# The small Pool products of a state-space layer, issued on the vector engine

## The chip, the core and the metric

One core of a Trainium2 chip. The engines that matter here are PE (TensorE, matrix products and transposes), DVE (VectorE), ACT (ScalarE), POOL (GpSimd) and SP, whose queue issues every DMA. Each engine works through its own list of instructions in order and waits on semaphores for the others. The metric is the device time of one execution in microseconds.

## The reference

A trunk of two layers on 1024 tokens of width 1024, in float32. In each layer the normed input is projected once; a slice `u` feeds a state-space (S5) group, the rest a differential attention with four heads. Both are concatenated and projected back, then a convolution-gated feed-forward follows.

```python
h = _rmsnorm(x, norm_mix[i]);  proj = h @ w_in[i]
y_ssm = _s5_group(u, lam_re, lam_im, log_step, b, c, d, w_glu, g_norm)   # 32 groups, 64 states, scan over 1024 tokens
y_att = _diff_attention_group(q, k, v, cos, sin, lam, lam_init, g_subln) # 4 heads, softmax pairs
x = x + jnp.concatenate([y_ssm, y_att], axis=-1) @ w_out[i]
x = x + _conv_gated_ffn(_rmsnorm(x, norm_ffn[i]), w_up[i], w_conv[i], b_conv[i], w_down[i])
```

The scan over tokens is not run step by step. From the poles (`lam_re`, `lam_im`, `log_step`) the kernel works out tables: powers of the pole for steps 0 to 8 times the input and output matrices, and rotations of the pole for 128 blocks of 8 tokens.

## The kernel before

Every float32 product on PE is three reduced-precision products (`mm3`, L399 to L402) on a high and a low part; ACT writes the high part and another engine subtracts it to get the low part. For weights this is `split` (L228 to L233), issued on POOL and giving tiles `op`, from a ring of nine slots (`W`).

At the start of a layer PE runs the projection: products `rw` for attention heads and `u` for the state-space input, in the order of `DENSE`. Beside them a background list (`Tasks`, ticked between groups of products) issues other work:

- `s5_prelude` works out poles and powers (`pt`) and the input matrix `Y` on DVE.
- `s5_rotations` (L634) makes four pairs of tables of 128x1024: products of an index row with the fine (`fl`) and the coarse (`fh`) part of the angle, a reduction to half a turn on DVE, sines on ACT, two stores.
- `s5_tables` (L657) runs 16 batches of two groups. In `first` three operations of 128x288 make `W4` (names `ws<-XC,pt` twice, then `ws<-ws`), six stores follow (`pk`), and three DVE operations of 128x256 make `Gt` (`ws<-Y,pt` twice, then `ws<-ws`). In `second`, one batch later, PE transposes `Gt` (L695, two) and multiplies `Y` by `W4` (L697, two) into a PSUM tile `w`; ACT copies it out, DVE adds `D8`, and `pw` and `kd` are stored.
- After that come the rotary turn of the first head (`ra`, `rb`, `qr`, `kr` on DVE), its transposes (`qt`, `kt`), and attention block by block: scores `sc` on PE, maxima `am` and `anm` on DVE, exponentials `e` on ACT, the weighted difference `e<-e,acf` on DVE, transposes `wt` on PE.

A scheduler under the kernel sets the order on each engine from the program and its own estimates; tiles come from pools of rotating buffers (`s4`: 40 buffers shared by almost all of these names), so that a new tile can wait for readers of an older one. An engine that waits holds up all that stands behind it on that engine.

Of the kernel before, what the change touches and what calls it, by code (L numbers as in the profile page):

```python
# [51 lines left out]
def trunk_kernel(ctx: ExitStack, tc: tile.TileContext, A: dict, out: bass.AP, dbg: dict):  # L52
    nc = tc.nc
    V, G, PE, dma = nc.vector, nc.gpsimd, nc.tensor, nc.sync.dma_start
# [11 lines left out]
    def s4(name):  # L66
        return P4.tile([128, 1024], F32, tag="s4", name=name)
# [10 lines left out]
    def bgt(name):  # L78
        return BG.tile([128, 512], F32, tag="bg", name=name)
# [17 lines left out]
    def act(o, i, f, **kw):  # L97
        return nc.scalar.activation(o, i, f, **kw)  # L98

    def tt(o, a, b, op):  # L100
        V.tensor_tensor(o, a, b, op=op)  # L101

    def ts(o, a, s1, s2, op0, op1):
        V.tensor_scalar(o, a, s1, s2, op0, op1)
# [4 lines left out]
    MUL, ADD, SUB = ALU.mult, ALU.add, ALU.subtract  # L109
# [7 lines left out]
    class Tasks:  # L117
# [3 lines left out]
        def store(self, dst, src):  # L121

            self.late.append((dst, src))
# [384 lines left out]
    def s5_prelude(l, P):  # L508
# [65 lines left out]
        ts(fh, f8, c17, -c17, ADD, ADD)  # L574
        tt(fl, f8, fh, SUB)
        P["rot"] = bg.add(s5_rotations(l, fh, fl, iota))

        Ar, Ai = (pt[:, c:c + 288].rearrange("p (t g) -> p t g", g=32) for c in (0, 288))
# [55 lines left out]
    def s5_rotations(l, fh, fl, iota):  # L634

        for q in range(4):
            p1, p2, p3 = s4("ph1"), s4("ph2"), s4("ph3")
            v1, v2 = (p.rearrange("p (g m) -> p g m", g=8) for p in (p1, p2))
            sh = [128, 8, 128]
            it = iota.unsqueeze(1).to_broadcast(sh)  # L640
            g8 = slice(8 * q, 8 * q + 8)
            G.tensor_tensor(v2, it, fl[:, g8].unsqueeze(2).to_broadcast(sh), op=MUL)
            tt(v1, it, fh[:, g8].unsqueeze(2).to_broadcast(sh), MUL)
            yield
            tt(p3, p1, p2, ADD)
            ts(p3, p3, MAGIC, -MAGIC, ADD, ADD)
            tt(p1, p1, p3, SUB)
            tt(p1, p1, p2, ADD)
            ts(p1, p1, 0.5, -0.5, ALU.min, ALU.max)
            yield  # L650
            act(p2, p1, AF.Abs)
            act(p1, p1, AF.Sin, scale=twopi_s)
            act(p3, p2, AF.Sin, scale=-TWO_PI, bias=halfpi)
            store(rt[l][q][0], p3)
            store(rt[l][q][1], p1)

    def s5_tables(l, P):  # L657
        Ar, Ai, XC, Y, D8 = (P[k] for k in ("Ar", "Ai", "XC", "Y", "D8"))

        def first(b):  # L660
            g2 = slice(2 * b, 2 * b + 2)
            ws = s4("ws")

            We, wt, Gt = ws[:, 0:288], ws[:, 288:576], ws[:, 576:832]
            W4, t4 = (v.rearrange("p (g t c) -> p g t c", g=2, c=16) for v in (We, wt))
            sh = [128, 2, 9, 16]
            ar = Ar[:, :, g2].rearrange("p t g -> p g t").unsqueeze(3).to_broadcast(sh)
            ai = Ai[:, :, g2].rearrange("p t g -> p g t").unsqueeze(3).to_broadcast(sh)
            G.tensor_tensor(W4, XC[:, 0, g2].unsqueeze(2).to_broadcast(sh), ar, op=MUL)
            G.tensor_tensor(t4, XC[:, 1, g2].unsqueeze(2).to_broadcast(sh), ai, op=MUL)  # L670
            G.tensor_tensor(We, We, wt, op=ADD)
            for g in range(2):
                o3 = pk[l][b][:, 128 * g:128 + 128 * g]
                ox = pk[l][b][:, 256 + 128 * g:384 + 128 * g]
                sw = W4[:, g, 1:9, :].rearrange("p t c -> p (t c)")
                store(o3, sw)
                store(ox[0:64], sw[64:128])
                store(ox[64:128], sw[0:64])

            wg = ws[:, 288:544]  # L680
            G4, h4 = (v.rearrange("p (g t c) -> p g t c", g=2, c=16) for v in (Gt, wg))
            sh = [128, 2, 8, 16]
            ar = Ar[:, 7::-1, g2].rearrange("p t g -> p g t").unsqueeze(3).to_broadcast(sh)
            ai = Ai[:, 7::-1, g2].rearrange("p t g -> p g t").unsqueeze(3).to_broadcast(sh)
            tt(G4, Y[:, 0, g2].unsqueeze(2).to_broadcast(sh), ar, MUL)
            tt(h4, Y[:, 1, g2].unsqueeze(2).to_broadcast(sh), ai, MUL)
            tt(Gt, Gt, wg, ADD)
            return b, W4, Gt, wg

        def second(b, W4, Gt, wg):  # L690
            o, q = b // 4, b % 4
            g2 = slice(2 * b, 2 * b + 2)
            ps = bgt("w1")
            for g in range(2):
                PE.transpose(ps[:, 128 * g:128 * g + 128], Gt[:, 128 * g:128 * g + 128], ident)  # L695
            for g in range(2):
                PE.matmul(ps[0:16, 256 + 128 * g:384 + 128 * g], Y[:, 0, 2 * b + g, :],  # L697
                          W4[:, g, 0:8, :].rearrange("p t c -> p (t c)"), start=True, stop=True)
            W1 = PW.tile([128, 2, 192], F32, tag="W1", bufs=3, name="W1")
            act(W1[:, :, 0:128], ps[:, 0:256].rearrange("p (g n) -> p g n", g=2), AF.Copy)  # L700
            act(W1[:, :, 128:192], ps[:, 0:256].rearrange("p (g n) -> p g n", g=2)[:, :, 0:64], AF.Copy)
            store(pw1[l][b], W1.rearrange("p g n -> p (g n)"))
            kp = wg[0:16].rearrange("p (g n) -> p g n", g=2)
            act(kp, ps[0:16, 256:512].rearrange("p (g n) -> p g n", g=2), AF.Copy)
            tt(kp[:, :, 0:16], kp[:, :, 0:16], D8.rearrange("p (g c) -> p g c", c=16)[:, g2, :], ADD)
            store(kd[l][o][:, 2 * q:2 * q + 2, 128:256], kp)

        held = []
        for b in range(16):
            held.append(first(b))  # L710
            yield
            if len(held) > 1:
                second(*held.pop(0))
        while held:
            yield 1
            second(*held.pop(0))
# [780 lines left out]
```

## Time and profile before

| | us |
|---|---|
| median of 3 runs | 2598.11 (2595.41 to 2607.71) |
| profiled execution | 2603.88 |
| its span, first to last instruction | 2602.1 |

| engine | busy, us | share of the span |
|---|---|---|
| PE | 2357.7 | 91% |
| DVE | 1747.9 | 67% |
| POOL | 1245.9 | 48% |
| ACT | 1131.7 | 43% |

The profile page gives busy time over the whole run; the stages differ. The two layers repeat each other: what stands at 62 to 220 us in the first layer stands at 1346 to 1490 us in the second. Times in the rows are microseconds from the start of the span. In a row of the chronological view the columns are start, length, engine, line, operation, output<-inputs, count, and in brackets how long the engine sat idle before it and who released it. An instruction's length there includes time in which it had started and could not proceed.

### The profile page before, as it was taken

The numbers are of one execution on the slowest core, as the hardware profiler recorded it, in microseconds if no ns is written. First come the engines' busy times: TensorE is split into PE (matmuls) and PEld (weight loads), VectorE is DVE, ScalarE is ACT, GpSimd is POOL, SyncE is SP. The second block draws the span as 40 slices with busy tenths as digits, with TensorE's granted clock in tenths as the row PEclk, the third lists the DMA queues.
The fourth block names the chain that finished last, engine by engine and source line by source line (L and its number), as shares of the span: only waits on it lengthen the run. The fifth ranks groups of instructions, "written<-read, shape, count | busy, mean of one in ns | idle before, by whom it ended". The sixth has DMA issues, their size and how long they took to land. (4 is left out here: it accounts for less than half of the span.)

```text
span 2602.1 us, 34422 instructions
## 1 busy us (share of the span) xinstructions
PE 2357.7 (91%) x12180; PEld 1948.0 (75%) x12180; DVE 1747.9 (67%) x3145; ACT 1131.7 (43%) x2164; POOL 1245.9 (48%) x957
## 2 busy tenths in 40 slices
PE   6689999997999999787996898999989999979888
PEld 5667987776888887566786688877768888866666
DVE  7977657758444444899588875676674444469985
ACT  4355346434544444333334542653344444433331
POOL 2741001026777776766237310011467777765761
PEclk8889999998999999899998999999999999999999
DMA  5334641321323223431234357214122322252311
GB/s 164 107 108 123 183 128 45 134 88 57 90 73 97 73 84 112 153 130 65 74 98 138 98 139 207 82 49 150 65 73 73 97 74 81 90 200 92 105 42 65
DMA packets 269828, 266.99 MB, mean 103 GB/s; under 512 B 40280, under 2 KB 227256, under 8 KB 269656
## 3 DMA queue, kind: packets, MB, share of 16 engines
q1 hardware_dynamic: 269656, 264.79, 32.8%
q8 instruction: 96, 1.57, 0.2%
q14 instruction: 76, 0.62, 0.1%
HBM read 188.17 MB, written 76.55 MB: 102 GB/s over the span
## 5 line engine op out<-in xcount | busy, mean ns | idle before, releaser
L232 POOL TENSOR_TENSOR op<-st,op 128x512 fp32r<-128x512 f32 x112 | 163.8, 1480 | 703.5 <-ACT op L98 661.3
L232 POOL TENSOR_TENSOR op<-wu,op 128x512 fp32r<-128x512 f32 x220 | 286.9, 1314 | 266.5 <-ACT op L98 266.2
L107 DVE SCALAR_TENSOR_TENSOR c<-u,cv,c 128x1023 f32<-128x1023 f32 (+1 forms) x176 | 227.2, 1291 | 61.9 <-ACT c L98 57.0
L400 PE MATMUL rw<-op,hTh 128*128 128x256 f32 x768 | 231.4, 301 | 5.4 <-ACT hTh L98 3.5
L232 POOL TENSOR_TENSOR op<-wd,op 128x512 fp32r<-128x512 f32 x106 | 156.1, 1489 | 161.7 <-ACT op L98 151.9
L401 PE MATMUL rw<-op,hTh 128*128 128x256 f32 x768 | 227.7, 296 | 1.2 <-POOL op L232 1.2
L402 PE MATMUL rw<-op,hTl 128*128 128x256 f32 x768 | 226.1, 295 | 0.0
L400 PE MATMUL dnc<-op,aop 128*128 128x512 f32 x360 | 155.7, 434 | 77.2 <-DVE xf L101 74.8
L101 DVE TENSOR_TENSOR u<-u,upc 128x512 f32<-128x512 f32 x88 | 60.1, 683 | 234.6 <-ACT u L98 234.5
L232 POOL TENSOR_TENSOR op<-w,op 128x512 fp32r<-128x512 f32 x124 | 170.0, 1390 | 41.1 <-ACT op L98 36.2
L98 ACT ACTIVATE op<-wu 128x512 fp32r<-128x512 f32 x220 | 138.0, 629 | 97.2 <-PE upd L402 57.6
L400 PEld LDWEIGHTS rw<-op,hTh 128*128 128x128 f32 x768 | 154.4, 201 | 9.3 <-ACT hTh L98 3.9
L400 PEld LDWEIGHTS dnc<-op,aop 128*128 128x128 f32 x360 | 71.9, 200 | 117.5 <-DVE xf L101 95.3
L401 PEld LDWEIGHTS rw<-op,hTh 128*128 128x128 f32 x768 | 154.5, 201 | 2.9 <-POOL op L232 2.0
L402 PEld LDWEIGHTS rw<-op,hTl 128*128 128x128 f32 x768 | 154.4, 201 | 1.1 <-issue 1.0
L98 ACT ACTIVATE op<-wd 128x512 fp32r<-128x512 f32 x106 | 66.5, 631 | 198.6 <-PE dnc L402 140.1
L101 DVE TENSOR_TENSOR xf<-xf,dnc 128x512 f32<-128x512 f32 (+1 forms) x160 | 123.8, 788 | 43.1 <-PE dnc L402 42.0
L98 ACT ACTIVATE u<-upa 128x512 f32<-128x512 f32 x132 | 78.6, 596 | 168.0 <-PE upa L402 168.0
L401 PE MATMUL dnc<-op,aop 128*128 128x512 f32 x360 | 148.4, 412 | 0.0
L402 PE MATMUL dnc<-op,aop 128*128 128x512 f32 x360 | 145.7, 413 | 1.1 <-DVE aop L232 1.0
L98 ACT ACTIVATE c<-u,cv 128x1024 f32<-128x1024 f32 x88 | 106.4, 1211 | 32.5 <-DVE u L101 29.7
L915 DVE TENSOR_REDUCE am<-sc 128x1 f32<-128x256 f32 (+7 forms) x128 | 94.3, 751 | 32.8 <-PE sc L913 32.5
(342 smaller groups left out, 7276.7 us busy)
## 6 DMA issues: line engine op xcount, KB each, us to landing
wu<-in_w_up_dram SPq DMA_DIRECT2D x88, 512.0 KB, 4.8
gd<-g SPq DMA_DIRECT2D x44, 512.0 KB, 3.1
wd<-in_w_down_dram SPq DMA_DIRECT2D x44, 512.0 KB, 4.2
g<-gd SPq DMA_DIRECT2D x44, 512.0 KB, 5.6
st<-in_w_in_dram SPq DMA_DIRECT2D x32, 256.0 KB, 4.4
st<-in_w_in_dram SPq DMA_DIRECT2D x16, 512.0 KB, 4.7
rt<-ph SPq DMA_DIRECT2D x16, 512.0 KB, 3.6
C<-rt SPq DMA_DIRECT2D x64, 128.0 KB, 2.8
```

The lines of the kernel that those rows point to most:

```text
L98: return nc.scalar.activation(o, i, f, **kw)
L101: V.tensor_tensor(o, a, b, op=op)
L107: return V.scalar_tensor_tensor(o, a, s, b, op0, op1)
L232: eng.tensor_tensor(lo.bitcast(F32R), src, hi, op=SUB)
L400: PE.matmul(o, l[0], r[0], start=first, stop=False, skip_group_check=go_on)
L401: PE.matmul(o, l[0], r[1], start=False, stop=False, skip_group_check=go_on)
L402: PE.matmul(o, l[1], r[0], start=False, stop=last, skip_group_check=go_on)
L915: V.tensor_reduce(out=m[:, c:c + 1], in_=sv, axis=AX.XY, op=ALU.max)
```

## The change

Four lines issue their operation on DVE instead of POOL: the product with the fine angle part in `s5_rotations` (four a layer, 128x1024) and the three operations that make `W4` in `s5_tables` (48 a layer, 128x288). In all 104 instructions change engine; what is computed is the same.

```diff
@@ s5_rotations
-            G.tensor_tensor(v2, it, fl[:, g8].unsqueeze(2).to_broadcast(sh), op=MUL)
+            tt(v2, it, fl[:, g8].unsqueeze(2).to_broadcast(sh), MUL)
             tt(v1, it, fh[:, g8].unsqueeze(2).to_broadcast(sh), MUL)
@@ s5_tables, first
-            G.tensor_tensor(W4, XC[:, 0, g2].unsqueeze(2).to_broadcast(sh), ar, op=MUL)
-            G.tensor_tensor(t4, XC[:, 1, g2].unsqueeze(2).to_broadcast(sh), ai, op=MUL)
-            G.tensor_tensor(We, We, wt, op=ADD)
+            tt(W4, XC[:, 0, g2].unsqueeze(2).to_broadcast(sh), ar, MUL)
+            tt(t4, XC[:, 1, g2].unsqueeze(2).to_broadcast(sh), ai, MUL)
+            tt(We, We, wt, ADD)
```

Since the scheduler places instructions anew, the order on the engines shifts with it. On DVE, in the first layer, around the first batch (`ws_1166`; `ph1_1134`, `ph2_1135`, `ph3_1136` belong to the second rotation table):

```order
-L101 TENSOR_TENSOR ws_1166<-Y_1021,pt_621 128x256 x2
+L101 TENSOR_TENSOR ws_1166<-XC_820,pt_621 128x288 x2
+L101 TENSOR_TENSOR ws_1166<-Y_1021,pt_621 128x256
+L101 TENSOR_TENSOR ws_1166<-ws_1166 128x288
 L101 TENSOR_TENSOR ph3_1136<-ph1_1134,ph2_1135 128x1024
+L101 TENSOR_TENSOR ws_1166<-Y_1021,pt_621 128x256
+L104 TENSOR_SCALAR ph3_1136<-ph3_1136 128x1024
 L101 TENSOR_TENSOR ws_1166<-ws_1166 128x256
```

The three new operations stand between and ahead of those that make `Gt`, for which PE's transposes wait. On PE the transposes of a batch move behind more products of the projection (`w1_1258` is the PSUM tile of the first batch, `rw_1225` a projection tile):

```order
-L695 MATMUL w1_1258<-ident_78,ws_1166 128x128 x2
-L697 MATMUL w1_1258<-ws_1166,Y_1021 16x128 x2
 L400 MATMUL rw_1225<-op0_314,hTh_511 128x256
...
 L400 MATMUL rw_1225<-op2_320,hTh_529 128x256
+L695 MATMUL w1_1258<-ident_78,ws_1166 128x128 x2
+L697 MATMUL w1_1258<-ws_1166,Y_1021 16x128 x2
 L401 MATMUL rw_1225<-op2_320,hTh_529 128x256
```

They stand 13 products later than before, those of the second and third batch 39 and 58 products later; when the first `qt` comes, PE has passed six batches in both orders. In the second layer 49 products more stand ahead of the first `qt` than before. A third place is DVE's list after the change at the first attention block (`am_1840`, `anm_1841`), where the thirteenth batch (`ws_1901`) stands:

```order
L915 TENSOR_REDUCE am_1840<-sc_1851 128x1
L101 TENSOR_TENSOR ws_1901<-XC_820,pt_621 128x288 [waits Pool_49]
L104 TENSOR_SCALAR anm_1841<-am_1840 128x1 [waits DVE_49]
L101 TENSOR_TENSOR ws_1901<-XC_820,pt_621 128x288
L101 TENSOR_TENSOR ws_1901<-Y_1021,pt_621 128x256
L101 TENSOR_TENSOR ws_1901<-ws_1901 128x288 [waits DVE_49]
```

Here the buffer that `ws_1901` gets was last read by a split on POOL, so DVE waits for POOL with the block's `anm` behind it; before, the waits for buffers of `ws` stood on POOL.

## Rows read from the trace of the kernel before

**Rows 1.** Windows: PE, PEld, DVE, ACT, POOL busy (instructions), clock, DMA share, GB/s

```profile
62.00:140.00 78.00, 53.20 (x367) 48.07 (x367) 72.65 (x139) 26.65 (x58) 57.72 (x48) 0.85 0.33 99
140.00:171.30 31.30, 24.21 (x166) 20.05 (x166) 25.50 (x54) 15.54 (x38) 15.41 (x17) 0.92 0.36 110
171.30:220.00 48.70, 47.77 (x265) 36.58 (x266) 38.02 (x105) 30.46 (x84) 11.53 (x12) 0.94 0.36 100
1346.50:1415.00 68.50, 48.21 (x330) 43.52 (x328) 64.33 (x112) 24.06 (x49) 52.27 (x35) 0.86 0.29 97
1415.00:1450.00 35.00, 29.87 (x218) 25.80 (x217) 29.53 (x55) 18.23 (x45) 20.29 (x21) 0.99 0.34 109
```

**Rows 2.** Waits of PE (60:300, 1360:1600: total, times, longest); two chronological PE rows

```profile
PE w L695 <- DVE ws L101: 22.0, 5, 8.1
...
PE w L695 <- DVE ws L101: 20.3, 5, 7.5
...
89.52 0.69 PE L695 MATMUL w<-ident,ws 128*128 128x128 f32 x2 [8.11 <-DVE ws L101]
...
171.34 0.48 PE L943 MATMUL wt<-ident,e 128*128 128x128 f32 x1 [3.81 <-DVE anm L104]
```

**Rows 3.** Chronological rows of POOL, then of DVE, 62 to 67 us

```profile
61.96 1.94 POOL L642 TENSOR_TENSOR ph<-D,pt 128x1024 f32<-128x1024 f32 x1 [23.67 <-DVE am L104]
64.75 1.89 POOL L642 TENSOR_TENSOR ph<-D,pt 128x1024 f32<-128x1024 f32 x1
...
62.03 1.91 DVE L101 TENSOR_TENSOR t<-am,lrt 128x32 f32<-128x32 f32 x1
63.97 2.72 DVE L101 TENSOR_TENSOR pt<-pt 128x32 f32<-128x32 f32 x1
```

**Rows 4.** Chronological rows of DVE beside an idle POOL

```profile
89.99 0.41 DVE L101 TENSOR_TENSOR ws<-Y,pt 128x256 f32<-128x256 f32 x1
90.33 1.21 DVE L101 TENSOR_TENSOR ph<-ph,ph 128x1024 f32<-128x1024 f32 x1
```

**Rows 5.** DVE groups: 62:171 (three), 28:62 (one), 1346.5:1450 (two); whole run (min/median/max)

```profile
L101 DVE TENSOR_TENSOR ws<-Y,pt 128x256 f32<-128x256 f32 x26 | 14.2, 563 | 1.8 <-POOL ws L671 1.5 <-PE qt L858 0.2
L107 DVE SCALAR_TENSOR_TENSOR r<-rd_k,r 128x32 f32<-128x32 f32 x18 | 11.0, 610 | 0.2
...
L104 DVE TENSOR_SCALAR nl<-nl 128x1 f32<-128x1 f32 x1 | 0.1, 141 | 0.0
...
L107 DVE SCALAR_TENSOR_TENSOR r<-rd_k,r 128x32 f32<-128x32 f32 x4 | 0.8, 192 | 0.1
...
L101 DVE TENSOR_TENSOR ws<-Y,pt 128x256 f32<-128x256 f32 x26 | 18.7, 737 | 6.3 <-POOL ws L671 4.6 <-PE qt L858 1.2 <-issue 0.3
L101 DVE TENSOR_TENSOR ph<-ph,ph 128x1024 f32<-128x1024 f32 x12 | 18.3, 1522 | 0.0
...
L101 DVE TENSOR_TENSOR ws<-Y,pt x64: 405/414/1514, 86.2 to 1469.7; 128x256 f32<-128x256 f32 x64
```

**Rows 6.** POOL groups of 62:171 and 1346.5:1450: the splits; one split beside little else

```profile
L232 POOL TENSOR_TENSOR op<-st,op 128x512 fp32r<-128x512 f32 x11 | 22.5, 2060 | 7.8 <-ACT op L98 7.7
...
L232 POOL TENSOR_TENSOR op<-st,op 128x512 fp32r<-128x512 f32 x12 | 21.3, 1788 | 8.3 <-ACT op L98 8.3
...
1498.87 1.27 POOL L232 TENSOR_TENSOR op<-st,op 128x512 fp32r<-128x512 f32 x1 [2.60 <-ACT op L98]
```

**Rows 7.** Chronological rows of POOL: its longest waits ahead of a batch's first product

```profile
143.07 0.70 POOL L669 TENSOR_TENSOR ws<-XC,pt 128x288 f32<-128x288 f32 x1 [7.65 <-DMA kd<-ws]
156.06 0.94 POOL L669 TENSOR_TENSOR ws<-XC,pt 128x288 f32<-128x288 f32 x1 [10.52 <-PE qt L858]
183.69 0.70 POOL L669 TENSOR_TENSOR ws<-XC,pt 128x288 f32<-128x288 f32 x1 [8.30 <-PE wt L943]
...
1433.23 0.94 POOL L669 TENSOR_TENSOR ws<-XC,pt 128x288 f32<-128x288 f32 x1 [8.76 <-PE qt L858]
1461.14 0.70 POOL L669 TENSOR_TENSOR ws<-XC,pt 128x288 f32<-128x288 f32 x1 [8.13 <-DMA st<-in_w_in_dram]
```

## Prediction before the run

> **What bounds the kernel now.** I read the busy times first, then the windows of the stage that holds the changed lines, then PE's waits, then DVE and POOL side by side. Over the run PE is busy 91%, so a gain must come from time in which PE stands still. In the stretch where the tables are made PE is busy only 53.2 of 78.0 us, and in the second layer 48.2 of 68.5, while DVE is busy 72.7 and 64.3 [rows 1]. Right behind, from 171 to 220 us, PE is busy 47.8 of 48.7 [rows 1]: there PE is the bound. PE's waits name the reason: transposes L695 for a batch's `Gt` wait for DVE, 22.0 us in the first layer and 20.3 in the second, five waits each; the first is 8.1 us, and the last wait of this stage that DVE causes is for the weighted difference at 171.3 us [rows 2]. So **DVE's list, from 62 to 171 us and from 1346 to 1450 us, sets the pace**, and the sum has to be made on DVE.
>
> Much of DVE's busy time there is no work. At 62.03 us a product of 32 columns lasts 1.91 us and ends at 63.94; POOL's product L642 beside it runs from 61.96 to 63.90. The next one to show it, at 63.97, lasts 2.72 us and ends at 66.69, with POOL's second L642 ending at 66.64 [rows 3]. Such a small product takes about 0.19 us where POOL is idle. DVE is held while POOL has an operation in flight.
>
> **The change part by part.**
>
> *What DVE gets.* Lengths overlap by 0.07 us: the 256-column product at 89.99 lasts 0.41 and the next starts 0.34 later [rows 4]. No row shows 288 columns on DVE. From 0.34 a step for 256 columns and 1.21 - 0.07 = 1.14 for 1024 [rows 4] a column costs (1.14 - 0.34)/768 = 1.04 ns, and 288 columns 0.37 us. By the first weighted difference DVE's new list has passed 13 of the 16 batches and all four angle products: 39 x 0.37 = 14.4 and 4 x 1.14 = 4.6, **19.0 us a layer**. The bounds are close: 0.34 and 0.44 a step (the latter if nothing overlaps) give 17.8 and 21.7.
>
> *What DVE loses.* I compare each group of DVE instructions in the window 62 to 171 with its length where POOL is idle. The 18 steps `r` of the angle reduction average 610 ns against 192: 7.5 us. The 26 products `ws<-Y,pt` average 563 against a median of 414: 3.9 us. Done for all 55 groups of this window, from the largest down to the single `nl` step of 141 ns, the excess is **34.4 us**. In the second layer the same comparison gives 34.1, with 26 x (737 - 414) = 8.4 from `ws<-Y,pt` and 12 x (1522 - 1210) = 3.7 from `ph<-ph,ph` as its first terms (1210 being the 128x1024 step of rows 4) [rows 4, 5]. POOL is busy 57.7 + 15.4 = 73.1 us in these stretches of the first layer, 22.5 of them with splits that stay; in the second 72.6 and 21.3 [rows 1, 6]. If the holding goes by POOL's busy time, 69% and 71% of it leave with the moved operations: **23.8 and 24.2 us**. DVE's own waits for `ws` from POOL, 1.5 and 4.6 us [rows 5], go too, because producer and consumer then share a list.
>
> *The sum on DVE.* First layer 19.0 - 23.8 - 1.5 = -6.3; second 19.0 - 24.2 - 4.6 = -9.8; together **-16.1 us**. PE follows it one to one as long as it waits for DVE in these stretches, which is where it loses time now; its new order lets it do 13 to 58 products before a transpose that waited, so that nothing on PE itself stands against it. Its clock is at 0.85 of full there, between the two levels 1.2 and 2.4 GHz; I give that no term, since a PE that waits for DVE gains nothing by running faster between waits.
>
> *Behind that point.* Three batches a layer are left, 9 x 0.37 = 3.3 us on DVE, where DVE is busy 38.0 of 48.7 us and PE nearly always [rows 1]: between 0 and 3.3 a layer, I take 1, so +2 in all.
>
> *POOL's waits that come along.* A batch's first product waits until its buffer is free. On POOL that cost nothing: 7.65, 10.52 and 8.30 us in the first layer, 8.76 and 8.13 in the second, 43.4 together [rows 7]. On DVE such a wait holds the rotary turn, the maxima and the differences queued behind. It costs between 0 and 43.4. I take 0: POOL ran ahead of DVE, while DVE reaches these batches later by itself, and in the new order the tenth batch's wait for `qt` stands behind DVE work that needs the same `qt`.
>
> *POOL's gain* is worth nothing by itself: the splits for weights run up to nine slots ahead of PE, and the waits of PE in rows 2 are not for them.
>
> Sum: -16.1 + 2 = **-14 us**. The profiled execution took 2603.88 us (span 2602.1 and 1.8 around it), 5.8 above the median of 2598.11; it becomes about 2590, and the median 2584.
>
> One rule is weighed here. The split of the holding above rests on busy time; the two rows at 62 us show a DVE product held to the end of POOL's operation. The Trainium skill, "SBUF — State Buffer", section "Who interferes with whom", says that a DVE instruction with two SBUF inputs and a POOL instruction that reads SBUF exclude each other, and that the second to issue blocks fully until the first ends. The rows at 62 us agree [rows 3]. By that rule taken in full each remaining split could hold DVE for its whole length when alone, 1.27 us: 11 and 12 splits give 14.0 and 15.2 us in place of the 10.6 and 9.9 that I leave standing, and the sum would be -14 + 8.7 = -5 us, 2593.
>
> **The rivals.**
>
> *A. Little is left of it* (2593; -2 to -10 us). The splits stay and find a DVE with more two-input products to collide with; if each holds DVE for its full 1.27 us, 8.7 us of the gain are lost, as worked out from rows 6. For it: POOL's splits already last 2060 and 1788 ns on average against 1.27 alone, so they meet DVE often. Against it: of the 73.1 us POOL is busy, DVE's excess is only 34.4, so a POOL operation costs DVE less than its length.
>
> *B. Slower: the buffer waits move onto DVE* (2608). The place is the first attention blocks: the thirteenth batch waits for a split on POOL, that one for ACT and for PE to be done with a ring slot, and `anm` stands behind it; the ninth to fourteenth batches wait for stores of earlier ones, which share SP's queue. If DVE meets a bit more than half of the 43.4 us [rows 7], some 24 us, the total is -14 + 24 = +10. From 14 us of such waits on the change loses. Against it: all of these waits end by things that themselves run behind DVE.
>
> *C. More: PE's waits go almost entirely* (2560). The new order puts 58 products ahead of the third batch's transposes and 49 more ahead of the second layer's first `qt`. If the waits at L695, 42.3 us [rows 2], nearly all go, the total is -38. Against it: DVE's list, at 19.0 us more work, still has to pass before the rotary turn.
>
> *D. It does not do what it says* (2635). If DVE's excess is not POOL's doing, 19.0 us are added twice and little is taken away: 38 + 2, less 0 to 6.1 of DVE's waits for `ws`, is +34 to +40. The rows at 62 us speak against it [rows 3].
>
> **How the numbers follow.** Forecast, -10 to -25 us: 0.45, at 2584. A: 0.26. B: 0.15. C: 0.11. D: 0.03. A measurement of this kernel tells a difference of about 0.5%, 13 us, from none. The forecast lies mostly beyond that (seven parts in ten, 0.32), and with C, 0.11, makes 0.43 for faster. Slower by over 13 us are D and half of B, 0.03 + 0.08 = 0.11. The rest, 0.46, is within the bound: A, the other half of B and the smaller values of the forecast. The likeliest single value stays 2584, just beyond the bound. The range, 2566 to 2606, takes in the forecast, A, the lower part of B and the nearer part of C; left out are some 0.07 of C, 0.09 of B and D's 0.03. The bounds of the unknown costs fit: the price of 288 columns moves the sum by -2 to +6, the last three batches by -2 to +5.
>
> **What would show it.** Right, if in the changed profile the 18 steps `r` average under 400 ns, the new `ws<-XC,pt` products take about 0.44 us, PE's waits at L695 fall below 15 us a layer, and the first one below 4; POOL's busy time falls by about 117 us while DVE's changes by less than 15. A is it if the steps `r` stay near 500 ns beside splits. B is it if DVE shows idle times before `ws<-XC,pt` released by POOL, PE or a DMA. C is it if PE is busy over 65 of the 78 us. The prediction is wrong at its root if DVE's excess stays with POOL nearly empty, or if PE stands idle elsewhere by as much as it gains here.

## The result

The changed kernel took 2573.05 us (median of 4 runs, 2572.01 to 2576.36); the kernel before, beside it on the same chip, took 2601.59 us (4 runs, 2595.41 to 2607.71). The ratio is 0.9886, with a 95% interval from 0.9869 to 0.9904: 28.5 us less, clear of the 0.5% that a measurement of this kernel can tell from no change. The profiled execution's span fell from 2602.1 to 2571.4 us. The sign and the range held; the size, -14 us, was half of what came, which lies beyond the forecast's -10 to -25 us and short of rival C's -38.

### The profile after

The windows of the changed kernel, cut at the same events as in [rows 1] (the first rotary transposes, the first `wt`), columns as there; the last two rows are the second layer's:

```profile
62.00:128.60 66.60, 51.18 (x376) 46.41 (x375) 63.89 (x176) 28.70 (x61) 35.05 (x16) 0.87 0.32 102
128.60:156.10 27.50, 26.44 (x175) 21.86 (x174) 26.41 (x68) 16.29 (x40) 6.19 (x4) 0.95 0.42 132
156.10:205.00 48.90, 45.43 (x262) 35.78 (x263) 39.77 (x118) 31.10 (x83) 5.11 (x4) 0.97 0.39 106
1331.00:1396.20 65.20, 50.71 (x380) 47.31 (x379) 56.56 (x146) 26.95 (x56) 34.06 (x8) 0.88 0.31 102
1396.20:1423.00 26.80, 25.72 (x175) 21.73 (x173) 25.68 (x65) 16.61 (x40) 6.23 (x4) 0.97 0.41 129
```

The stage of the first layer, 109.3 us long before, now takes 94.1. DVE, with 39 more products of 288 columns and 4 of 1024 in it, is busy for 90.3 us where it was busy for 98.2: it does more work in less busy time. The groups of the first layer's stage (62 to 156 us), columns as in [rows 5]:

```profile
L101 DVE TENSOR_TENSOR ws<-XC,pt 128x288 f32<-128x288 f32 x26 | 11.9, 474 | 0.0
L101 DVE TENSOR_TENSOR ws<-Y,pt 128x256 f32<-128x256 f32 x26 | 10.4, 409 | 0.1
L101 DVE TENSOR_TENSOR ph<-D,pt 128x1024 f32<-128x1024 f32 x8 | 9.6, 1207 | 0.0
L107 DVE SCALAR_TENSOR_TENSOR r<-rd_k,r 128x32 f32<-128x32 f32 x18 | 4.3, 236 | 0.0
```

The steps `r` average 236 ns against 610 before, `ws<-Y,pt` 409 against 563, and no idle time stands ahead of the new `ws<-XC,pt`. PE's waits in the two stages (60 to 300 us, then 1330 to 1600; total, times, longest):

```profile
PE w L695 <- DVE ws L101: 15.4, 5, 4.8
...
PE rw L401 <- POOL op L232: 10.0, 1, 10.0
...
PE w L695 <- ACT ph L98: 1.9, 1, 1.9
```

In the first layer the waits for `ws` fell from 22.0 to 15.4 us. In the second they are nearly gone (20.3 before), but a wait stands there that the trace of before does not have: 10.0 us for a split on POOL (before, no wait of PE for a split of the projection was over 0.7 us). The reason is in the group of POOL's splits, first layer and second:

```profile
L232 POOL TENSOR_TENSOR op<-st,op 128x512 fp32r<-128x512 f32 x12 | 41.0, 3442 | 63.7 <-ACT op L98 63.7
...
L232 POOL TENSOR_TENSOR op<-st,op 128x512 fp32r<-128x512 f32 x12 | 40.3, 3391 | 60.1 <-ACT op L98 60.1
```

With almost nothing else on POOL a split lasts 3.4 us, longer than the 2060 and 1788 ns of [rows 6], and 1.27 alone. The chronological rows of the second layer show one of them (POOL, then DVE beside it, then PE):

```profile
1352.65 9.34 POOL L232 TENSOR_TENSOR op<-st,op 128x512 fp32r<-128x512 f32 x1 [34.19 <-ACT op L98]
1361.95 12.41 POOL L232 TENSOR_TENSOR op<-st,op 128x512 fp32r<-128x512 f32 x1
...
1352.57 0.67 DVE L104 TENSOR_SCALAR ph<-ph 128x1024 f32<-128x1024 f32 x1
1353.17 0.41 DVE L101 TENSOR_TENSOR ws<-ws 128x256 f32<-128x256 f32 x1
...
1359.63 1.20 DVE L101 TENSOR_TENSOR ph<-D,pt 128x1024 f32<-128x1024 f32 x1
1360.76 1.27 DVE L101 TENSOR_TENSOR ws<-ws,D 16x32 f32<-16x32 f32 x1
...
1366.95 0.17 DVE L101 TENSOR_TENSOR ws<-ws,D 16x32 f32<-16x32 f32 x1
...
1372.03 1.21 DVE L101 TENSOR_TENSOR ph<-D,pt 128x1024 f32<-128x1024 f32 x1
...
1374.42 0.58 PE L401 MATMUL rw<-op,hTh 128*128 128x256 f32 x1 [10.04 <-POOL op L232]
```

From 1352.57 to 1360.76 DVE runs 13 instructions back to back at their undisturbed lengths, and the split that started at 1352.65 ends only at 1361.99. In its last 1.2 us it is DVE that is held: an add of 32 columns, 0.17 us at 1366.95, lasts 1.27. So POOL got its turn only at this add, after 8 us. The next split waited the same way: the add at 1366.95 did not let it in, DVE ran out of work at 1373.24, the split ended at 1374.36, and PE stood behind it. The holding works both ways: before, a busy POOL held DVE; now an unbroken DVE holds POOL.

To count it, each instruction of the stage (62 us to the first `wt`; the second layer's likewise) is compared with the length that 15% of its group (same operation and shape, in the two traces together) stay under. What it lasts longer is DVE's excess; beside it stands DVE's idle time (gaps of over 0.15 us), in us:

| kernel | excess, layer 1 | excess, layer 2 | idle, layer 1 | idle, layer 2 |
|---|---|---|---|---|
| before | 34.8 | 34.0 | 10.3 | 9.1 |
| changed | 7.8 | 3.8 | 3.2 | 9.1 |

### The profile page after: what moved, and what is told of

Same layout as the page of the kernel before. It is cut to its first block, busy times and chain, and to the rows that moved or that the text cites. A ratio compares the mean times of both kernels' runs of the same rounds, so it can differ in the third digit from the quotient of the medians.

```text
span 2571.4 us, 34399 instructions
## 1 busy us (share of the span) xinstructions
PE 2348.4 (91%) x12180; PEld 1945.3 (76%) x12180; DVE 1725.8 (67%) x3249; ACT 1134.1 (44%) x2164; POOL 1168.7 (45%) x853
## 5 line engine op out<-in xcount | busy, mean ns | idle before, releaser
L232 POOL TENSOR_TENSOR op<-st,op 128x512 fp32r<-128x512 f32 x112 | 199.8, 1806 | 850.1 <-ACT op L98 782.1
L401 PE MATMUL rw<-op,hTh 128*128 128x256 f32 x768 | 226.0, 294 | 10.5 <-POOL op L232 10.5
L400 PE MATMUL rw<-op,hTh 128*128 128x256 f32 x768 | 227.9, 297 | 6.9 <-ACT hTh L98 3.5
L401 PEld LDWEIGHTS rw<-op,hTh 128*128 128x128 f32 x768 | 151.9, 198 | 13.0 <-POOL op L232 11.3
L98 ACT ACTIVATE e<-sc,anm 128x256 f32<-128x256 f32 (+7 forms) x128 | 93.8, 736 | 49.4 <-DVE anm L104 36.3
```

Of the source, the lines that this page charges most:

```text
L232: eng.tensor_tensor(lo.bitcast(F32R), src, hi, op=SUB)
L400: PE.matmul(o, l[0], r[0], start=first, stop=False, skip_group_check=go_on)
L401: PE.matmul(o, l[0], r[1], start=False, stop=False, skip_group_check=go_on)
```

## The experiments

The theory: a POOL operation in flight holds DVE, so what the change gains is the holding that leaves, less the work that DVE gets. The rivals: the gain comes from the new order (the three products and their readers on one list, the transposes later on PE), or the splits that stay set the rest.

### One part alone

`e1_angle` issues only L642 on DVE:

```diff
-            G.tensor_tensor(v2, it, fl[:, g8]..., op=MUL)
+            tt(v2, it, fl[:, g8]..., MUL)
```

> Only the angle product L642 goes to DVE (8 instructions in all); the three W4 products stay on POOL. Theory of holding (a POOL product in flight holds DVE): 18.0 of the 116.7 us of moved POOL time leave, 15 percent of the 57 us of excess that the whole change removed, 9 us; DVE gets 8 x 1.14 = 9 us of work: no difference, 2595 to 2607. Theory of order (the gain comes from W4 and its reader standing on one list): no difference either. A gain of 10 us or more would say that a few long POOL operations hold DVE for more than their share.

Measured: 2597.82 us, ratio 0.9976 (0.9963 to 0.9988), beside 2604.09 of before: -6 us, within the expected 2595 to 2607.

`e2_w4` issues only L669 to L671 on DVE.

> Only the three W4 products go to DVE (96 instructions); L642 stays on POOL. Theory of holding: 85 percent of the 57 us of excess leave, 48 us, the work added is 78 x 0.37 = 29 us, DVE's waits for ws go (6 us): -25 us, about 2577. If L642 is what holds DVE most, at the stage's start: -15 us or less, 2587 or more.

Measured: 2578.91 us, ratio 0.9900 (0.9880 to 0.9919): -25 us. That is what the theory of holding expected. Together the parts give -31 us, about the whole; the angle product gives a fifth of it, with 15% of the moved POOL time. The steps `r` in the stage, for the first and the second kernel:

```profile
L107 DVE SCALAR_TENSOR_TENSOR r<-rd_k,r 128x32 f32<-128x32 f32 x18 | 8.3, 461 | 0.1
...
L107 DVE SCALAR_TENSOR_TENSOR r<-rd_k,r 128x32 f32<-128x32 f32 x18 | 5.4, 302 | 0.0
```

610, 461, 302, 236 ns: the less POOL does, the shorter DVE's small steps. The order theory has no reason for that, but it is not excluded by these two.

### The four products left out

`e4_left_out` is the kernel before without them: W4's stores and products read a piece of `Y`, and the rotations add the index row.

```diff
-            G.tensor_tensor(v2, it, fl[:, g8]..., op=MUL)
...
-            tt(p3, p1, p2, ADD)
+            tt(p3.rearrange("p (g m) -> p g m", g=8), v1, it, ADD)
...
-            G.tensor_tensor(W4, XC[:, 0, g2]..., ar, op=MUL)
-            G.tensor_tensor(t4, XC[:, 1, g2]..., ai, op=MUL)
-            G.tensor_tensor(We, We, wt, op=ADD)
```

> The kernel before with the four POOL products left out: W4's stores and products read a piece of Y, the rotations add the index row instead of the fine part. Theory of holding: DVE is free of the moved operations and has no work for them; the steps r average under 250 ns; of the 38 us that these products cost DVE in the changed kernel it gains what PE's remaining waits in the two stages allow, 15.4 + 15 = 30 us: 2540 to 2550. Theory of order, with no holding: DVE's work is that of before, only its waits for ws (6 us) go: 2592 to 2602.

Measured: 2552.71 us, ratio 0.9804 (0.9788 to 0.9820). That is 51 us less than before, 3 us short of the 2540 to 2550 that the theory of holding expected; the order theory's 2592 to 2602 is far off. Against the changed kernel's ratio of 0.9886 the difference is 0.8%, some 21 us: what the 38 us of products cost when DVE does them. So the operations on POOL cost 51 us, on DVE 21, each with what hangs on them (the stores of `pk` no longer wait for them). The steps `r` missed the expected 250 ns, at 366, and the excess was 10.5 and 8.0 us, more than in the changed kernel. The splits last 2327 ns there in the first layer, where they last 3442 in the changed kernel: beside fewer products on DVE they get in sooner. Why they do was not isolated.

### One-input copies in place of the products

`e5_pool_copy` keeps four POOL operations of the same size, but as copies (the second factor and the sum are left out):

```diff
-            G.tensor_tensor(v2, it, fl[:, g8]..., op=MUL)
+            G.tensor_copy(v2, fl[:, g8]...)
...
-            G.tensor_tensor(We, We, wt, op=ADD)
+            G.tensor_copy(We, wt)
```

> The kernel before with the four POOL products replaced by POOL copies of the same size with one input (the second factor and the sum are left out). If any POOL operation in flight holds DVE, by its busy time: the steps r stay at 500 to 600 ns and the time follows the copies' busy time, 2585 to 2605 if they are about as long as the products. If only operations with two inputs on both engines exclude each other: r falls to 200 to 260 ns, and the time is near that of the kernel without the products, 2540 to 2560.

Measured: 2574.36 us, ratio 0.9884 (0.9868 to 0.9899), `r` at 338 ns, between the two expectations. The chronological rows tell why (POOL, then DVE):

```profile
62.79 1.09 POOL L642 COPY ph<-pt 128x1024 f32<-128x1024 f32 x1 [24.52 <-DVE am L104]
63.82 0.94 POOL L502 MEMSET zero<- 16x1024 f32 x1
64.72 1.03 POOL L642 COPY ph<-pt 128x1024 f32<-128x1024 f32 x1
...
62.87 1.05 DVE L101 TENSOR_TENSOR t<-am,lrt 128x32 f32<-128x32 f32 x1
63.84 0.17 DVE L101 TENSOR_TENSOR t<-am,lit 128x32 f32<-128x32 f32 x1
63.95 1.84 DVE L101 TENSOR_TENSOR pt<-pt 128x32 f32<-128x32 f32 x1
```

A copy with one input holds DVE just as long as it lasts; it is only shorter, 1.03 us for 1024 columns where the product of [rows 3] took 1.89 to 1.94. So it is not a matter of two inputs on POOL. The product at 63.95 is held through the MEMSET, which reads nothing, and the copy behind it; the one at 63.97 in [rows 3] began beside the same MEMSET and was held through the product behind it. A MEMSET with nothing behind it is found in the changed kernel (POOL, then DVE); the last two rows are the same DVE instructions in `e4_left_out`, with POOL idle:

```profile
46.86 0.94 POOL L502 MEMSET zero<- 16x1024 f32 x1 [9.06 <-DVE hn L107]
...
47.26 0.28 DVE L101 TENSOR_TENSOR lamv<-lamv 128x128 f32<-128x128 f32 x1
47.45 0.43 DVE L104 TENSOR_SCALAR gs<-gs 128x128 f32<-128x128 f32 x1
...
47.47 0.28 DVE L101 TENSOR_TENSOR lamv<-lamv 128x128 f32<-128x128 f32 x1
47.67 0.22 DVE L104 TENSOR_SCALAR gs<-gs 128x128 f32<-128x128 f32 x1
```

The product with two inputs takes 0.28 us beside the MEMSET as without it; the TENSOR_SCALAR is held until the MEMSET ends. The Trainium skill, "SBUF — State Buffer", section "Who interferes with whom", says that a DVE instruction with two SBUF inputs doesn't contend with a GpSimd instruction that only writes. The row at 47.26 agrees, and the product at 63.84 above passed beside the MEMSET too. The rows at 63.95 and 63.97 don't settle it, since in both a POOL operation with inputs follows the MEMSET at once; what held these two products from their start stays open.

### POOL made busy again

Is it POOL's activity by itself? `e6_extra_pool` adds to the changed kernel four POOL products a batch that nobody reads, in spare columns of `ws`:

```diff
+            for _ in range(4):
+                G.tensor_tensor(ws[:, 832:1024], xf[:, 0:192], xf[:, 192:384], op=MUL)
             tt(G4, Y[:, 0, g2]..., ar, MUL)
```

> The changed kernel with four POOL products of 128x192 a batch added whose results nobody reads: same work and same order of dependences on DVE, only POOL is busy again (64 a layer, some 30 us). Theory of holding, POOL over DVE: DVE's steps r are back at 400 us or more in ns, the excess rises by the added POOL time of the stage, some 20 us a layer, and the time to 2600 to 2615. Theory that DVE's unbroken stream keeps POOL out: the added products stretch instead, DVE's lengths stay, and the time is 2573 to 2585, with longer waits of PE for splits queued behind them. Theory of order: no difference, 2573.

Measured: 2614.76 us, ratio 1.0041 (1.0026 to 1.0056). The time went where the theory of holding had it, but not by its way alone: `r` stood at 256 ns. The groups of the first layer's stage, DVE and POOL, then chronological rows of POOL and one of DVE:

```profile
L101 DVE TENSOR_TENSOR ws<-XC,pt 128x288 f32<-128x288 f32 x26 | 13.1, 520 | 9.8 <-POOL op L232 9.8
L107 DVE SCALAR_TENSOR_TENSOR r<-rd_k,r 128x32 f32<-128x32 f32 x18 | 4.6, 256 | 0.0
...
L687 POOL TENSOR_TENSOR ws<-XC 128x192 f32<-128x192 f32 x55 | 57.5, 1053 | 17.9 <-ACT XC L98 14.8
...
110.53 16.91 POOL L687 TENSOR_TENSOR ws<-XC 128x192 f32<-128x192 f32 x1
...
135.35 28.65 POOL L687 TENSOR_TENSOR ws<-XC 128x192 f32<-128x192 f32 x34
163.96 5.37 POOL L232 TENSOR_TENSOR op<-st,op 128x512 fp32r<-128x512 f32 x4
...
165.26 1.50 DVE L101 TENSOR_TENSOR ws<-XC,pt 128x288 f32<-128x288 f32 x1 [9.78 <-POOL op L232]
```

DVE's excess rose to 17.2 and 22.2 us, but beside it stand waits for POOL ahead of `ws<-XC,pt`, 9.8 and 8.3 us: in the first layer the split that DVE waits for stands on POOL behind 34 of the added products. It is the prediction's rival B, made by hand. The run doesn't tell the two apart, so a second one adds POOL work without that tie: in `e7_extra_own` two products a batch write spare columns of `D8`'s tile (`pad`), and nothing on DVE needs them.

```diff
+            for _ in range(2):
+                G.tensor_tensor(P["pad"], xf[:, 0:192], xf[:, 192:384], op=MUL)
             tt(G4, Y[:, 0, g2]..., ar, MUL)
```

> The changed kernel with two POOL products of 128x192 a batch added (32 a layer, 0.6 us each, 19 us) whose result goes to spare columns that nobody reads, so that no work on DVE waits for them; they run in one row from the moment XC is there (62 us). Theory of holding, POOL over DVE: in the first 25 us DVE's lengths grow by most of the 19 us, the first transposes of the stage come 10 to 19 us later than in the changed kernel (84.5 us), and the time is 2595 to 2611. Theory that DVE's stream keeps POOL out: the added products stretch to over 1 us on average, DVE's excess grows by under 6 us a layer, and the time rises only by what splits queued behind cost: 2575 to 2590.

Measured: 2598.85 us, ratio 0.9983 (0.9974 to 0.9993). PE's waits in the first layer (L698 is the changed kernel's L695), POOL's row, and DVE's small steps beside it:

```profile
PE w L698 <- DVE ws L101: 26.7, 5, 15.7
...
62.44 29.42 POOL L687 TENSOR_TENSOR D<-XC 128x192 f32<-128x192 f32 x29 [23.91 <-ACT XC L98]
...
63.18 0.59 DVE L101 TENSOR_TENSOR t<-pt,lrt 128x32 f32<-128x32 f32 x1
64.37 0.17 DVE L104 TENSOR_SCALAR pt<-t 128x32 f32<-128x32 f32 x1
65.24 0.58 DVE L104 TENSOR_SCALAR pt<-t 128x32 f32<-128x32 f32 x1
```

DVE's work and its order are the changed kernel's, instruction by instruction; only POOL is busy with some 19 us a layer that nobody needs (32 products of 0.59 us at the shortest). The first transposes of the stage come at 99.04 us in place of 84.46, DVE's excess is 23.1 and 22.9 us in place of 7.8 and 3.8, and almost the whole gain of the change is gone: 25 us. That is the holding measured by itself. With the new order but a busy POOL only 3 us of gain are left, so the order alone is not the reason. It may still have a part: DVE's idle time is 2.3 and 1.2 us here, where before had 10.3 and 9.1. With the holding that left (34.8 - 23.1 and 34.0 - 22.9) this about pays for the 19.0 us of work that DVE gets in each layer. Whether the order or DVE's longer list took these waits away was not separated.

### The splits that stay

`e3_split_dve` issues the twelve splits of the stage on DVE too (`plain` gets an engine: the second head's and both state-space parts):

```diff
-                plain([(wcols(w, 0, 8, 256 * i, 256), 0)])
+                plain([(wcols(w, 0, 8, 256 * i, 256), 0)], V)
...
+                      V if i == 1 else G)
```

> The changed kernel with the weights' splits of three projection parts (the second head and both state-space parts, 12 a layer, those that POOL runs in the table stage) issued on DVE as well. In the changed kernel they last 3.4 us on average on POOL, DVE's stream keeps them out, and PE waits 10.0 us for one in the second layer. Theory that the holding is mutual and that a held split is what is left: PE's 10.0 us go, DVE's rest of excess (7.8 and 3.8 us) goes, and DVE gets 12 x 0.62 = 7.4 us a layer: 2560 to 2568. Theory that POOL's splits are hidden and PE would have waited for DVE anyway: the added 7 us a layer come out in full, 2580 to 2588.

`e3b_split_h1` does so for the second head's four alone, among them the one for which PE waited.

> The changed kernel with only the second head's four splits a layer on DVE, among them the one for which PE waited 10.0 us. Mutual holding: PE's wait goes, DVE gets 4 x 0.62 = 2.5 us a layer: 2562 to 2569, as good as moving all twelve or better. If PE's wait only moves to the transposes behind it: 2573 to 2578.

`after_again` is the changed kernel beside them.

> The changed kernel once more, on the same chip as the others of this set, as their measure: 2570 to 2577.

Measured: 2561.61 us for all twelve (ratio to before 0.9841, 0.9824 to 0.9857; the theory that a held split is what is left had 2560 to 2568), 2576.63 for the four (0.9893, 0.9877 to 0.9910), 2573.36 for the changed kernel (0.9881, 0.9866 to 0.9895). All twelve on DVE bring 12 us more and make the fastest kernel that computes the reference here: DVE's excess falls to 1.6 and 1.4 us, its idle time to 1.3 and 0.9. A split takes there (group of the first layer's stage) 0.68 us, about half of its 1.27 on an undisturbed POOL:

```profile
L232 DVE TENSOR_TENSOR op<-st,op 128x512 fp32r<-128x512 f32 x10 | 6.5, 675 | 0.2 <-ACT op L98 0.2
L107 DVE SCALAR_TENSOR_TENSOR r<-rd_k,r 128x32 f32<-128x32 f32 x18 | 3.1, 175 | 0.0
```

The four alone brought nothing, against the theory's 2562 to 2569: the wait moved, as the other expectation had it, and the way is worth following. Second layer, POOL's splits; the wait of SP's queue; ACT; PE:

```profile
1362.63 30.73 POOL L232 TENSOR_TENSOR op<-st,op 128x512 fp32r<-128x512 f32 x3 [1.52 <-ACT op L98]
...
SPq L331 <- POOL op L232: 10.6, 1, 10.6
...
1398.34 0.55 ACT L98 ACTIVATE W<-w 128x256 f32<-128x256 f32 x2 [7.98 <-DMA pw<-W]
...
1399.19 1.11 PE L868 MATMUL kt<-ident,kr 128*128 128x128 f32 x4 [7.92 <-ACT ws L98]
```

Three of the splits left on POOL were kept out for 30.73 us. A weight load on SP's queue waits 10.6 us for one of them to be done with its source tile; the stores of the tables stand behind it, ACT waits for the store of `W` to free its buffer, and PE's `kt` stands behind ACT. The 10.0 us of the changed kernel became 7.9 at another place.

## Why the prediction came out as it did

- **The bound and the mechanism** were right: DVE's list sets the pace, and POOL's operations hold DVE. `e7_extra_own` and `e4_left_out` show it.
- **What DVE gets**, 19.0 us a layer, was right by the rows: from 1354.64 to the next start at 1355.01 a product of 288 columns advances the list by 0.37 us.
- **What DVE loses** was mis-sized: 23.8 and 24.2 us by the share of POOL's busy time, 27.0 and 30.2 by the same comparison (34.8 - 7.8 and 34.0 - 3.8). The step that failed is that the splits would go on to hold DVE for their share. They found a DVE without gaps and were held themselves. 10.6 and 9.9 us were left standing for them; 7.8 and 3.8 are what was found. Rival A, and the sum by the Trainium skill's rule that stands with it, went wrong at the same place: they let each split block DVE for 1.27 us, while most of the time it stood outside.
- **DVE's waits** were mis-sized both ways. I counted the waits for `ws` from POOL alone, 1.5 and 4.6. In the first layer DVE's idle time fell by 7.1 us, since waits for ACT's products went too. In the second it fell by nothing: 8.6 of the 9.1 us after are waits for ACT's `ws`, behind the PE that waited 10.0 us for a split.
- **The sums with the measured terms** close. That is in part bookkeeping, since the stage's length is DVE's work, excess and idle time together; what the closing confirms is the 19.0 us of work. First layer: 19.0 - 27.0 - 7.1 = -15.1; the first `wt` moved from 171.34 to 156.05, -15.3 (predicted -6.3). Second: 19.0 - 30.2 - 0 = -11.2; the `wt` moved by 1449.98 - 1423.02 = 27.0, of which 15.6 were brought along from the first layer, leaving -11.3 (predicted -9.8). The second layer came out near its forecast by luck: 6.0 us more holding left than predicted, and the 4.6 us of waits did not.
- **Behind that point** I took +1 a layer; from the first `wt` to the conv tables' product (`cv`) it was -1.3 and -1.4, but 0.0 and +0.3 in `after_again`, the same kernel once more: executions differ by as much, and no cause is shown. The rest is 0.9 us lost and 2.3 gained in the feed-forward stages, which the change doesn't touch; from the second layer's `cv` to the end the kernels here take 961.1 to 964.4 us, a difference of 3.3, and I leave that unexplained. In all -15.3 - 1.3 + 0.9 - 11.3 - 1.4 - 2.3 = -30.7, the difference of the spans.
- **POOL's buffer waits**, taken at 0, were 0.0 in the stage; rival B did not come.
- **POOL's gain is worth nothing** was wrong in its reason. I held the splits to be covered by the nine slots of the ring; in the second layer PE waited 10.0 us for one. It was late because DVE kept POOL out. The wait is there in `after_again` too, with 9.0 us.
- **The marks**: `r` under 400 ns and the products at 0.44 us held; PE's waits at L695 were 15.4 us in the first layer where I wrote under 15, the first of them 1.4 us (under 4). POOL's busy time fell by 77.2 us, not 117, and DVE's by 22.1 us instead of staying within 15: both are the exchange of who is held.

## What to carry to other kernels

Where DVE sets the pace, a POOL operation beside it is not free: compare its length on POOL with its length on DVE (here 1.9 us against 1.14 for the same product), and move it over if DVE is the faster. In these runs a microsecond of such work cost about as much on either engine: 21 us for 38 on DVE, 25 for 38 in `e7_extra_own`, and 51 for some 72 on POOL (an estimate from the shortest lengths of before, 8 x 1.89 and 26 batches x (0.69 + 0.70 + 0.79)). Then look at what stays on POOL: small work with a deadline, such as a split that PE or a load on SP's queue waits for, can be kept out by an unbroken DVE stream. Here four of twelve splits moved brought nothing, all twelve brought 12 us. A wait that is moved out of PE's way in one queue can come back through the queue behind it.

## What the runs showed of the hardware

- A POOL instruction can stand for 8 us and more with DVE working beside it: 9.34 and 12.41 us for splits of 1.27, and 30.73 for three. What lets POOL into DVE's stream was not isolated. At 1360.76 it was an add that needs ACT's copy, at 1366.95 an add of the same kind passed without letting it in. In `e7_extra_own`, where POOL had 29 products in a row and DVE many small dependent steps, the two took turns and no product lasted more than 1.63 us; in `e6_extra_pool` one such product stood for 16.91 us.
- DVE instructions with one input are held too: the TENSOR_SCALAR of 32 columns at 65.24 in `e7_extra_own` lasted 0.58 us, one of the same kind at 64.37 lasted 0.17; the one of 128 columns beside a MEMSET 0.43 in place of 0.22.
- A POOL copy of 1024 columns takes 1.03 us where POOL's product takes 1.94, and holds DVE for just that time. A MEMSET alone held a TENSOR_SCALAR of DVE but not a product with two inputs (0.28 us beside it and without it).
